# Hybrid DeltaNet and attention layer on one core: modulation rows moved, bias corners set once, paired products in the inverse, the last head's output spread out

## The chip, the cores and the metric

The kernel runs on one core of a Trainium2 chip. The metric is the device time of one execution in microseconds (us). Three executions of the kernel before took 2202.82, 2208.03 and 2638.72 us; the median is 2208.03 us. The profiled execution took 2206.4 us, of which the trace covers a span of 2204.7 us.

## The reference: what is computed

One layer on 1024 tokens of width 1024, all in float32:

```python
mod = (silu(c) @ w_ada + b_ada)                    # 6 x 1024: shift, scale, gate, twice
h = x * (1 + scale_t) + shift_t
proj = h @ w_in                                    # 9232 columns
o_a = gated_deltanet(q, k, v, z, beta, a)          # 8 heads of 128, chunks of 64
o_b = chunk_band_attention(q, k, v, rel_bias)      # 16 heads of 64, own chunk and 8 before
merged = gate_a * (o_a @ w_branch_a) + gate_b * (o_b @ w_branch_b)
x = layernorm(alpha * x + gate_t * (merged @ w_o))
h = x * (1 + scale_f) + shift_f
u_gate, u_val = split(causal_dwconv(h @ w_up) + b)
x = layernorm(alpha * x + gate_f * ((silu(u_gate) * u_val) @ w_down))
```

The DeltaNet heads solve a unit lower triangular system for each chunk of 64 rows. The attention adds a relative-position bias to the scores; a frame sees no key outside its band, which the kernel expresses by a large negative number (`NEG`) in two 64x64 corners of the bias tile.

## The kernel before, in words

Every large product is made from two parts of each operand, a high part (the float32 value cast to fp32r) and a low part (what the cast left). A product is three matmuls: high x high, low x high, high x low. So each weight block that is loaded into a buffer `raw` (a ring of three, 512 KB each) is cast on ScalarE (ACT), which gives `wh`, and its low part `wl` is the difference, taken on GpSimd (POOL, lines 177 and 188) or VectorE (DVE, line 177). All loads and stores are issued by SyncE (SP) in program order.

The stages, in order of time:

- 0 to about 100 us: the first part of the modulation, the layer's input, the first projections.
- About 100 to 800 us: the eight DeltaNet heads. The loop over h = 0 to 6 (line 934) runs, for head h, the solve and the recurrence, while `feed(h + 1)` (line 681) makes the next head's projections, short convolution, Gram matrices and the rows that the solve reads; it also makes some blocks of the merge gates (`gate_block`) and of the attention's q and k (`qk_block`), taken from the iterator `gates`. `feed` yields after each few matmuls and says how many units they were. The loop's `waves` are streams with a position in units: a wave is run when the feed has come so far. Waves are `stage_inverse` (line 767, four pieces), `stage_chain` (line 811, the recurrence) and `stage_out` of the head before (line 846; tiles `pt`, `sz`).
- `stage_solve` (line 744) is forward substitution on VectorE in 32 rows: a product (line 751) and a reduction (line 753) per row on a tile that the ring calls FT, a transpose (line 755), then copies of blocks (line 763) and transposes (line 765). `stage_inverse` joins the 32x32 blocks into 64x64 ones by small matmuls: `pxt` and `py` for the 32x32 blocks, then `pzz` and `pT`, sixteen of 64x64 each. There are two small products per step for `pxt`, which lie in two different quarters of the partitions.
- `mod_rows(cb)` (line 898) makes 512 of the later modulation's 4096 columns: four loads of 512 KB of `w_ada` into the ring `raw`, eight VectorE operations that sum them over the rows (lines 907 and 909), one matmul `pmod` with ones, a bias row and a store. Rows of 512 are numbered 0 to 7. `feed(h + 1)` makes row h in its second half, and in the fourth head row 7 as well (`HM = 3`).
- About 800 to 1310 us: the last DeltaNet head and then the attention's 64 groups (16 heads of 4 groups, the loop of `g` at line 1261). Both are filled with a second stream, `fills`: the remaining q and k blocks (`pqk`), the values (`pv`), the load of branch A's input (`branch_a_in`, line 1064: eight loads of 512 KB with cast and low part), and branch A's eight weight blocks (`branch_a(j)`, line 1074). `FILL` and `SHARE` say how many units lie between the steps of a group.
- A group's scores `ps` get the bias and their exponentials' sums on VectorE and ACT (lines 1153 to 1159), GpSimd divides by the sum (line 1160, tile G, widths 128 to 640), TensorE transposes (`pp`), ACT casts and VectorE makes the low part `pl` (line 1182), and TensorE makes the output `po`.
- `Head.bias` (line 993) loads one head's bias into a tile of a ring of two (G as well), in two pieces (line 997), and sets two corners to `NEG` by GpSimd (lines 998 and 999). `Head.keys` (line 980) casts the first head pair's keys twice on ACT, once to each half of the partitions (lines 982 and 983), and takes the low part on VectorE (line 984).
- About 1240 to 1350 us: the rest of branch A (`pbr`). With j = 5, 6 and 7 the attention's output is read back from `ob_d` through `raw`, cast and split. Then branch B (line 1304, `mm_fm`, `pbr` at line 286), the output product, the normalisation, the up product (line 1515, seven products in place of eight) and the down product (line 1669), to 2205 us.

Instructions are put in order by a scheduler with a timeline of its own; in the loop of the heads, in the last head and in the attention the matmuls are kept in the order in which the program has them (`lane.pinned`), and every engine keeps the order that the build gives it.

Of the kernel before, what the change touches and what calls it, by code (L numbers as in the profile page):

```python
# [17 lines left out]
P = 128  # L18
S = 1024
D = 1024  # L20
NK = 8
# [16 lines left out]
HM = 3  # L38
# [7 lines left out]
MS = 6  # L46
FILL = (120, 124, 100, 112, 125, 130, 140, 110)
# [90 lines left out]
def hybrid_layer(  # L138
# [542 lines left out]
    def feed(h, n_gates, mods):  # L681
# [36 lines left out]
        if mods[1:]:  # L718
            run(mod)
            mod = mod_rows(mods[1])  # L720
            next(mod)
# [22 lines left out]
    def stage_solve(h, c):  # L744

        fa = c["fa"]
        ft = ring("ft", [P, 8, 32])
        POOL.tensor_copy(ft, tt0)
        for i in range(1, 32):
            pr = ring("pr", [P, 8, 32])  # L750
            DVE.tensor_tensor(pr[:, :, 0:i + 1], ft[:, :, 0:i + 1],  # L751
                              fa[:, i:i + 1, 0:i + 1].to_broadcast([P, 8, i + 1]), ALU.mult)
            DVE.tensor_reduce(ft[:, :, i:i + 1], pr[:, :, 0:i + 1], AX.X, ALU.add, negate=True)  # L753
        fr = ring("pr", [P, 8, 32])
        DVE.transpose(fr.rearrange("p c j -> p (c j)"), ft.rearrange("p c j -> p (c j)"))
        for b in (1, 3, 0, 2):
            for q in range(4):
                dst = dd[B[b], :, 32 * b + 8 * q:32 * b + 8 * q + 8]
                s_ = fr[B[q], :, 8 * b:8 * b + 8].rearrange("p c t -> p t c")
                if q % 2:  # L760
                    ACT.copy(dst, s_)
                else:
                    DVE.tensor_copy(dst, s_)
        for b in (1, 3, 0, 2):
            DVE.transpose(dt_[B[b], :, B[b]], dd[B[b], :, B[b]])

    def stage_inverse(h, c):
# [31 lines left out]
        pz = ibank("pzz", 64)  # L799
        for u in range(NT):  # L800
            lane.matmul(pz[lo_, u], am[:, u, lo_], am[:, u, hi_], start=True, stop=True)
        ACT.activation(zd[lo_], pz[lo_], AF.Copy, scale=-1.0)
        POOL.memset(am[hi_, :, lo_], 0.0)
        yield
        pT = ibank("pT", 64)
        for u in range(NT):
            lane.matmul(pT[lo_, u], dd[:, u, lo_], zd[:, u], start=True, stop=True)
        DVE.tensor_copy(am[lo_, :, hi_], pT[lo_])
# [89 lines left out]
    def mod_rows(cb):  # L898

        C = slice(2 * D + 512 * cb, 2 * D + 512 * cb + 512)  # L900
        acc = ring("gt", [P, 512])
# [12 lines left out]
        row = ring("gt", [P, 512])[0:1, :]  # L914
# [5 lines left out]
    gates = iter([*range(1, 2 * NK), *((i,) for i in EP)])  # L920
# [13 lines left out]
    for h in range(HA - 1):  # L934
        fill, done = feed(h + 1, GA[h], (h, HA - 1)[:1 + (h == HM)]), 0
# [6 lines left out]
        i0 = INV0 if h else INV00  # L942
        waves += [(inv, i0 + INVS * i) for i in range(4)]
# [18 lines left out]
    vts, ma, keys_low = {}, {}, []  # L962

    class Head:
# [15 lines left out]
        def keys(self, N, src, at):  # L980
            kh, kl = self.kh, self.kl
            ACT.copy(kh[at:at + 64, N], src)
            ACT.copy(kh[64 - at:P - at, N], src)
# [9 lines left out]
        def bias(self):  # L993
            bt = self.bt = ring("bt", [P, 640])
            src = rel_d[self.h].rearrange("r s -> (r s)")[127:127 + 767 * P].rearrange("(p s) -> p s", p=P)
            for c in (slice(384, 640), slice(0, 384)):
                SP.dma_start(bt[:, c], src[:, c])
            POOL.memset(bt[0:64, 576:640], NEG)
            POOL.memset(bt[64:128, 0:64], NEG)
# [65 lines left out]
    def branch_a_in():  # L1065

        def body(_):
            for k in range(NK):
                load_split(oahk[k], oalk[k], oa_d[k], ACT, POOL if k in OL else DVE)
# [4 lines left out]
    def branch_a(j):  # L1074

        def body(w):
            ma[j] = place(MA[j], [P, S], F32, "ma")
            for n in range(2):
# [5 lines left out]
                DVE.scalar_tensor_tensor(gt_, gt_, 1.0, ps, ALU.add, ALU.mult)  # L1084
            for k in {5: (0, 1), 6: (2, 3, 4), 7: (5, 6, 7)}.get(j, ()):
# [146 lines left out]
    waves = [(older, OUT0 + OUTS * i) for i in range(3)]  # L1232
# [12 lines left out]
    for i, (stream, at_) in enumerate(waves):  # L1245
        if i == 7:
            group("GA", "G", 4096)
            head(0).bias()
# [11 lines left out]
    done, owed = 0, None  # L1260
    for g in range(8 * NK):
# [12 lines left out]
        if g == 0:  # L1274
            seq += [lambda: wave(last, PC)] * 3
# [521 lines left out]
```

## Time and profile before

| what | value |
|---|---|
| median of three executions | 2208.03 us |
| profiled execution | 2206.4 us |
| its span | 2204.7 us |
| granted TensorE clock, mean | 0.992 |
| TensorE busy | 2123.3 us, 11561 matmuls |
| VectorE busy | 1451.7 us |
| ScalarE busy | 981.7 us |
| GpSimd busy | 488.3 us |
| bytes moved | 258.78 MB, 38.0% of 16 DMA engines |

The page gives busy time by engine, then the span in 40 slices, the DMA queues, the chain of work that ended last, and the costliest groups by line. The view of waits lists, for each engine, what its idle time ended on: total us, times, longest. A timeline row is start, duration, engine, line, operation, output and inputs, and in brackets the idle time just before it with what ended it. Names are those of the program's buffers, so that many tiles of one ring share a name: `G` is the scores, the bias tiles and small pieces of the solve, `GT` the gates and the modulation's sums, `FT` the solve's rows, and later the ring `gb`.

### The profile page before, as it was taken

How to read it: one execution, taken by the hardware profiler on the slowest of the kernel's cores; microseconds unless marked ns; L12 is line 12 of the kernel's file. 1: busy time of each engine (PE TensorE's matmuls, PEld its weight loads, DVE VectorE, ACT ScalarE, POOL GpSimd, SP SyncE). 2: the span in 40 equal slices, each digit the busy share in tenths (PEclk: the TensorE clock that was granted, in tenths of full speed). 3: DMA queues.
4: the chain of work that ended last, by engine and by line, in shares of the span. 5: the costliest groups of instructions: out<-in, count | busy, mean ns of one | idle time of the engine just before them, and what ended most of it. 6: DMA issues, size and time to landing. Idle time of an engine off the chain costs nothing.

```text
span 2204.7 us, 32006 instructions
## 1 busy us (share of the span) xinstructions
PE 2123.3 (96%) x11561; PEld 1775.4 (81%) x11561; DVE 1451.7 (66%) x3112; ACT 981.7 (45%) x2129; POOL 488.3 (22%) x466
## 2 busy tenths in 40 slices
PE   7999999999999999998999899999999999999998
PEld 5787888877887878888888788888788888888886
DVE  6478586777767734655655553457997888875654
ACT  4544443443434433555555542234654444452331
POOL 0233223222232222332333423300120000000000
PEclk9999999999999999999999999999999999999999
DMA  9242324333234124535454633342232222275540
GB/s 291 75 130 63 117 75 118 127 92 115 82 106 129 51 75 134 146 95 134 121 142 131 170 122 97 112 133 87 85 97 86 68 86 77 96 261 207 172 153 38
DMA packets 239520, 258.78 MB, mean 117 GB/s; under 512 B 21818, under 2 KB 188147, under 8 KB 239363
## 3 DMA queue, kind: packets, MB, share of 16 engines
q1 hardware_dynamic: 239283, 256.72, 38.0%
q8 instruction: 91, 1.49, 0.3%
q14 instruction: 66, 0.54, 0.1%
q10 hardware_dynamic: 80, 0.03, 0.0%
HBM read 204.22 MB, written 58.76 MB: 119 GB/s over the span
## 4 chain that ended last, share of the span: by engine, by line
PE 78%; DVE 10%; DMA 5%; ACT 3%; POOL 2%; issue 2%; SPq 1%; DVEq 0%; ACTq 0%; POOLq 0%
PE pup L1515 17%; PE pdn L1669 11%; PE pqkv L528 9%; PE pqk L528 6%; PE pwo L1357 4%; PE pgt L528 4%; PE pbr L286 4%; PE pv L528 4%; PE pbr L528 4%; PE po L528 3%; PE pz L528 3%; DVE FT L751 2%; PE ps L528 2%; PE pp L528 2%; DVE FT L753 1%
## 5 line engine op out<-in xcount | busy, mean ns | idle before, releaser
L1515 PE MATMUL pup<-hh,wop 128*128 128x512 f32 x704 | 224.3, 390 | 0.4 <-ACT G L1552 0.4
L1515 PE MATMUL pup<-t,wop 128*128 128x512 f32 x792 | 189.5, 392 | 1.2 <-DVE cc L1556 0.7
L177 POOL TENSOR_TENSOR wl<-raw,wh 128x1024 fp32r<-128x1024 f32 x55 | 131.7, 2397 | 265.0 <-ACT wh L174 242.5
L1515 PEld LDWEIGHTS pup<-t,wop 128*128 128x128 f32 x792 | 148.6, 188 | 34.7 <-DVE cc L1556 1.1
L1669 PE MATMUL pdn<-dop,dop 128*128 128x512 f32 x696 | 161.6, 391 | 0.0
L1515 PEld LDWEIGHTS pup<-hh,wop 128*128 128x128 f32 x704 | 132.2, 188 | 29.1 <-ACT G L1552 0.8
L1669 PEld LDWEIGHTS pdn<-dop,dop 128*128 128x128 f32 x696 | 130.6, 188 | 28.3
L528 PE MATMUL pqkv<-hh,wh 128*128 128x512 f32 x352 | 144.0, 410 | 0.0
L528 PE MATMUL pqkv<-hl,wh 128*128 128x512 f32 x352 | 141.0, 401 | 0.0
L528 PE MATMUL pqkv<-hh,wl 128*128 128x512 f32 x352 | 140.8, 400 | 0.0
L1160 POOL TENSOR_SCALAR G<-G,ST 128x640 f32<-128x640 f32 (+4 forms) x128 | 86.4, 676 | 240.8 <-DVE ST L1159 180.3
L1515 PE MATMUL pup<-hl,wop 128*128 128x512 f32 x352 | 137.2, 390 | 0.0
L1557 POOL TENSOR_TENSOR cc<-cc,G 128x512 f32<-128x512 f32 x22 | 44.4, 2018 | 375.4 <-DVE G L1539 352.3
L1157 ACT ACTIVATE G<-G,ST 128x640 f32<-128x640 f32 (+4 forms) x128 | 89.3, 698 | 67.5 <-DVE ST L1153 66.5
L751 DVE TENSOR_TENSOR FT<-FT,G 128x16 f32<-128x16 f32 (+30 forms) x248 | 103.7, 418 | 12.8 <-POOL G L650 5.5
L528 PE MATMUL pqk<-hh,wh 128*128 128x512 f32 x256 | 106.8, 417 | 3.6 <-DVE GT L879 3.6
L174 ACT CAST wop<-wr 128x512 fp32r<-128x512 f32 x104 | 61.6, 620 | 97.4 <-DVE wr L1497 57.5
L528 PE MATMUL pqk<-hl,wh 128*128 128x512 f32 x256 | 104.7, 409 | 0.0
L528 PE MATMUL pp<-ident,G 128*128 128x128 f32 x480 | 78.8, 276 | 26.6 <-POOL G L1160 20.8
L528 PE MATMUL pqk<-hh,wl 128*128 128x512 f32 x256 | 104.2, 407 | 0.0
L528 PE MATMUL pgt<-hh,wh 128*128 128x512 f32 x240 | 98.2, 409 | 0.0
L528 PE MATMUL pgt<-hh,wl 128*128 128x512 f32 x240 | 97.6, 407 | 0.0
(403 smaller groups left out, 5665.8 us busy)
## 6 DMA issues: line engine op xcount, KB each, us to landing
raw<-in_w_in_dram SPq DMA_DIRECT2D x72, 512.0 KB
wr<-in_w_up_dram SPq DMA_DIRECT2D x44, 512.0 KB
dwr<-in_w_down_dram SPq DMA_DIRECT2D x44, 512.0 KB
raw<-in_w_ada_dram SPq DMA_DIRECT2D x32, 512.0 KB
qk_d<-FT SPq DMA_DIRECT2D x72, 128.0 KB
wa<-in_w_ada_dram SPq DMA_DIRECT2D x32, 256.0 KB
gates_d<-GT SPq DMA_DIRECT2D x32, 256.0 KB
g_d<-G SPq DMA_DIRECT2D x15, 512.0 KB
```

What stands on the lines that cost most here:

```text
L174: he.copy(h, src)
L177: return le.tensor_tensor(l, src, f(h), ALU.subtract).ins
L286: i = PE.matmul(ps, a[:, k, :], r[k][:, 512 * n:512 * n + 512], start=(k == 0 and a is wh and r is rh), stop=(k == NK - 1 and a is wl))
L528: r = getattr(PE, op)(*args, **kw)
L751: DVE.tensor_tensor(pr[:, :, 0:i + 1], ft[:, :, 0:i + 1], fa[:, i:i + 1, 0:i + 1].to_broadcast([P, 8, i + 1]), ALU.mult)
L753: DVE.tensor_reduce(ft[:, :, i:i + 1], pr[:, :, 0:i + 1], AX.X, ALU.add, negate=True)
L1157: ACT.activation(sb[:, 0:n], sb[:, 0:n], AF.Exp, bias=mx[:, nb - 1:nb], scale=-1.0, accum_out=mx[:, 2:3])
L1160: POOL.tensor_scalar(sb[:, 0:n], sb[:, 0:n], mx[:, 3:4], 0.0, ALU.mult, ALU.add)
L1357: PE.matmul(ps[n], a[:, t, k, :], wo[k][b][:, 512 * n:512 * n + 512], start=(k == 0 and a is mh and b == 0), stop=(k == NK - 1 and a is ml))
L1515: i = PE.matmul(ps, a[:, u, k, :], b[v][k], start=(new and k == 0 and u == 0 and v == 0), stop=(k == 3 and u == 1), skip_group_check=not new)
L1557: self.later(7, lambda: POOL.tensor_tensor(o, o, self.t, ADD))
L1669: PE.matmul(ps[n], self.g[:, u, i * P:i * P + P], self.w[v][:, 512 * n:512 * n + 512], start=(first and u == 0 and v == 0), stop=(last and ...
```

## The change

There are eight edits.

1. **Modulation.** `feed(h + 1)` makes row h - 1 for h = 1 to 6, so no row in head 1's feed, and one in each later one (0 to 5). Rows 6 and 7 are made in branch A: row 6's loads and sums start after block j = 4 and its matmul and store after j = 5, row 7 after j = 6 and j = 7. Their sums lie in the ring `gb`.
2. **Order of the blocks.** `gates` gives q and k blocks 4 and 12 after gate block 3 (in head 1's feed) and no longer at the end (in head 7's feed).
3. **Block copies.** `stage_solve` ends with the transpose of line 755; what follows (lines 756 to 765) is `stage_blocks`, a wave at position 0 of the head's own loop (22 units before the inverse for head 0).
4. **Paired products.** `pzz` and `pT` write the even of their sixteen products to partitions 0 to 63 and the odd ones to 64 to 127. Each result is then copied in two halves of 64 x 4 x 64, for `pzz` by two ACT operations in place of one, for `pT` by one on ACT and one on VectorE.
5. **Bias corners.** `bias()` issues four loads that leave the corners out, in place of two loads and two GpSimd operations. The corners of the ring's two tiles are set once, before head 0's bias.
6. **Keys.** The second ACT cast of `keys` is replaced by a copy by DMA from the first half.
7. **Last head's output.** Eight units of fill come before the attention's loop, and in group 0 the three pieces of the last `stage_out` stand between pieces of fill of four units, after the first turn.
8. **Low parts.** `branch_a_in` takes the low parts in two pieces of 512 columns (`cuts=2`).

```diff
-HM = 3
+HEAD0 = 8
@@ feed
-        if mods[1:]:
-            run(mod)
-            mod = mod_rows(mods[1])
-            next(mod)
@@ stage_solve, stage_blocks
-        fr = ring("pr", [P, 8, 32])
+        fr = c["fr"] = ring("pr", [P, 8, 32])
         DVE.transpose(fr.rearrange("p c j -> p (c j)"), ft.rearrange("p c j -> p (c j)"))
+
+    def stage_blocks(h, c):
+        fr = c["fr"]
         for b in (1, 3, 0, 2):
...
             DVE.transpose(dt_[B[b], :, B[b]], dd[B[b], :, B[b]])
+        yield
@@ stage_inverse
-        pz = ibank("pzz", 64)
+        sides = (lo_, hi_)
+        def pairs(name):
+            return mtile(nm(name), "i")[:, 0:256].rearrange("p (t d) -> p t d", d=64)
+        pz = pairs("pzz")
         for u in range(NT):
-            lane.matmul(pz[lo_, u], am[:, u, lo_], am[:, u, hi_], start=True, stop=True)
-        ACT.activation(zd[lo_], pz[lo_], AF.Copy, scale=-1.0)
+            lane.matmul(pz[sides[u % 2], u // 2], am[:, u, lo_], am[:, u, hi_], start=True, stop=True)
+        for i in range(2):
+            ACT.activation(zd[lo_, i::2], pz[sides[i]], AF.Copy, scale=-1.0)
...
-        pT = ibank("pT", 64)
+        pT = pairs("pT")
         for u in range(NT):
-            lane.matmul(pT[lo_, u], dd[:, u, lo_], zd[:, u], start=True, stop=True)
-        DVE.tensor_copy(am[lo_, :, hi_], pT[lo_])
+            lane.matmul(pT[sides[u % 2], u // 2], dd[:, u, lo_], zd[:, u], start=True, stop=True)
+        ACT.copy(am[lo_, 0::2, hi_], pT[lo_])
+        DVE.tensor_copy(am[lo_, 1::2, hi_], pT[hi_])
@@ mod_rows: acc and row from ring(key)
-    def mod_rows(cb):
+    def mod_rows(cb, key="gt"):
@@ gates and the loop of the heads
-    gates = iter([*range(1, 2 * NK), *((i,) for i in EP)])
+    gates = iter([1, 2, 3, *((i,) for i in EP), *range(4, 2 * NK)])
-        fill, done = feed(h + 1, GA[h], (h, HA - 1)[:1 + (h == HM)]), 0
+        fill, done = feed(h + 1, GA[h], (h - 1,) if h else ()), 0
+        waves = [(stage_blocks(h, cs[h]), 0)] + waves if h else [(stage_blocks(h, cs[h]), i0 - 22)]
@@ Head.keys, Head.bias
-            ACT.copy(kh[64 - at:P - at, N], src)
+            SP.dma_start(f(kh[64 - at:P - at, N]), f(kh[at:at + 64, N]))
-            for c in (slice(384, 640), slice(0, 384)):
-                SP.dma_start(bt[:, c], src[:, c])
-            POOL.memset(bt[0:64, 576:640], NEG)
-            POOL.memset(bt[64:128, 0:64], NEG)
+            for r, c in ((lo_, slice(384, 576)), (hi_, slice(384, 640)), (lo_, slice(0, 384)), (hi_, slice(64, 384))):
+                SP.dma_start(bt[r, c], src[r, c])
@@ branch_a_in, branch_a
-                load_split(oahk[k], oalk[k], oa_d[k], ACT, POOL if k in OL else DVE)
+                load_split(oahk[k], oalk[k], oa_d[k], ACT, POOL if k in OL else DVE, cuts=2)
+            if j in (4, 6):
+                mods_late.append(mod_rows(j // 2 + 4, "gb"))
+                next(mods_late[-1])
+            if j in (5, 7):
+                run(mods_late[-1])
@@ last head and group 0
-    waves = [(older, OUT0 + OUTS * i) for i in range(3)]
+    waves = [(stage_blocks(h, cs[h]), 0)] + [(older, OUT0 + OUTS * i) for i in range(3)]
-        if i == 7:
+        if i == 8:
             group("GA", "G", 4096)
+            for o in AT["bt"]:
+                corner = place(o, [P, 640], F32, "bt")
+                POOL.memset(corner[0:64, 576:640], NEG)
+                POOL.memset(corner[64:P, 0:64], NEG)
             head(0).bias()
+    fill_to(HEAD0)
-            seq += [lambda: wave(last, PC)] * 3
+            seq = [head(1).bias, T[0], lambda: fill_to(done + 4), lambda: wave(last, PC), lambda: fill_to(done + 4),
+                   lambda: wave(last, PC), lambda: wave(last, PC), lambda: fill_to(done + 4)]
```

**GpSimd's order in the attention.** This is GpSimd's queue from the corners of the third head's bias on, before and then after. `L1160` of before is `L1173` after; `wl` is a weight's low part.

```order
L998 MEMSET G_7233 64x64
L188 TENSOR_TENSOR wl_8245<-raw_8246,wh_8244 128x512 x2
L999 MEMSET G_7233 64x64
L1160 TENSOR_SCALAR G_7233<-G_7233,ST_7002 128x128
L1160 TENSOR_SCALAR G_7233<-G_7233,ST_7002 128x256
L1160 TENSOR_SCALAR G_7233<-G_7233,ST_7002 128x384
L1160 TENSOR_SCALAR G_7233<-G_7233,ST_7002 128x512
L1160 TENSOR_SCALAR G_7233<-G_7233,ST_7002 128x640 x2
L188 TENSOR_TENSOR wl_8252<-raw_8253,wh_8251 128x512 x2
L1160 TENSOR_SCALAR G_7233<-G_7233,ST_7002 128x640 x2
L998 MEMSET G_7233 64x64
L1160 TENSOR_SCALAR G_7233<-G_7233,ST_7002 128x128
```

```order
L188 TENSOR_TENSOR wl_8223<-raw_8224,wh_8222 128x512 x2
L1173 TENSOR_SCALAR G_7207<-G_7207,ST_6954 128x128
L1173 TENSOR_SCALAR G_7207<-G_7207,ST_6954 128x256
L1173 TENSOR_SCALAR G_7207<-G_7207,ST_6954 128x384
L1173 TENSOR_SCALAR G_7207<-G_7207,ST_6954 128x512
L1173 TENSOR_SCALAR G_7207<-G_7207,ST_6954 128x640 x2
L188 TENSOR_TENSOR wl_8230<-raw_8231,wh_8229 128x512 x2
L1173 TENSOR_SCALAR G_7207<-G_7207,ST_6954 128x640 x2
L1173 TENSOR_SCALAR G_7207<-G_7207,ST_6954 128x128
```

The two corner operations no longer stand ahead of a division or between two of them; the low parts and the divisions keep their order.

**TensorE's order at the last head's output.** TensorE's queue where group 0 begins, before and then after: `pqk` is fill, `pp` the transposes of group 0's probabilities, `pt` the last head's output transposed.

```order
L528 MATMUL pp_7814<-ident,G_7233 128x128 x3
L528 MATMUL pqk_7792<-hl,wh_7673 128x512
L528 MATMUL pqk_7792<-hh,wl_7674 128x512
L528 MATMUL pt_7822<-ident,at_6667 128x128 x4
L528 MATMUL pqk_7792<-hh,wh_7673 128x512
L528 MATMUL pqk_7792<-hl,wh_7673 128x512
L528 MATMUL pt_7830<-ident,at_6667 128x128 x4
```

```order
L528 MATMUL pp_7797<-ident,G_7207 128x128 x3
L528 MATMUL pqk_7770<-hh,wh_7651 128x512
L528 MATMUL pqk_7770<-hl,wh_7651 128x512
L528 MATMUL pqk_7770<-hh,wl_7652 128x512
L528 MATMUL pqk_7770<-hh,wh_7651 128x512
L528 MATMUL pt_7807<-ident,at_6643 128x128 x4
L528 MATMUL pqk_7770<-hl,wh_7651 128x512
L528 MATMUL pqk_7770<-hh,wl_7652 128x512
L528 MATMUL pqk_7770<-hh,wh_7651 128x512
L528 MATMUL pqk_7770<-hl,wh_7651 128x512
L528 MATMUL pt_7817<-ident,at_6643 128x128 x4
```

Between `pp` and the first `pt` stand four matmuls of fill in place of two, and between the two `pt` four in place of two; the eight units of `HEAD0` stand further ahead.

**SyncE's order at the end of branch A.** SyncE's queue up to branch B's first weight (the last row), before and then after; `raw` is the ring of three, `raw<-ob_d` the attention's output read back.

```order
L182 DMA raw_12827<-ob_d 128x1024
L1083 DMA ma_12909<-gates_d 128x512
L1083 DMA ma_12772<-gates_d 128x512 x2
L1083 DMA ma_12842<-gates_d 128x512 x2
L182 DMA raw_12897<-ob_d 128x1024
L1083 DMA ma_12909<-gates_d 128x512
L182 DMA raw_12831<-ob_d 128x1024
L1209 DMA ob_d<-ob_12227 128x512
L182 DMA raw_12964<-ob_d 128x1024
L1364 DMA B_1563_12677<-mod_d 16x128
L182 DMA raw_12837<-in_w_branch_a_dram 128x8x128
L182 DMA raw_12978<-in_w_branch_b_dram 128x8x128
```

```order
L912 DMA raw_12908<-in_w_ada_dram 128x2x512
L912 DMA raw_12912<-in_w_ada_dram 128x2x512
L925 DMA mod_d<-FT_12664 1x512
L912 DMA raw_12916<-in_w_ada_dram 128x2x512
L923 DMA FT_12664<-in_b_ada_dram 1x512
L182 DMA raw_12920<-ob_d 128x1024
L182 DMA raw_12924<-ob_d 128x1024
L182 DMA raw_12928<-ob_d 128x1024
L182 DMA raw_12992<-ob_d 128x1024
L182 DMA raw_12996<-ob_d 128x1024
L182 DMA raw_13000<-ob_d 128x1024
L182 DMA raw_13006<-in_w_branch_b_dram 128x8x128
```

Row 7's loads of `w_ada` now stand between block j = 7 and six of the reads of `ob_d`, row 6's stand ahead of block j = 6 (earlier than these rows), and all reads of `ob_d` stand ahead of branch B's first weight, where four of the eight followed it before.

More of the change, by code (lines that the diff above doesn't have):

```diff
@@ L896, in gate_block @@
         return halves("pgt", GC + j * P, use, pend.pop("g", None))
-    def mod_rows(cb):
+    def mod_rows(cb, key="gt"):
         C = slice(2 * D + 512 * cb, 2 * D + 512 * cb + 512)
-        acc = ring("gt", [P, 512])
+        acc = ring(key, [P, 512])
         for k0 in range(0, NK, 2):
@@ L913, in mod_rows @@
         lane.matmul(pr_, ones, acc, start=True, stop=True)
-        row = ring("gt", [P, 512])[0:1, :]
+        row = ring(key, [P, 512])[0:1, :]
         SP.dma_start(row, b_ada[:, C])
@@ L961, in hybrid_layer @@
     oalk = [oal[:, k, :] for k in range(NK)]
-    vts, ma, keys_low = {}, {}, []
+    vts, ma, keys_low, mods_late = {}, {}, [], []
     class Head:
@@ L994, in bias @@
             bt = self.bt = ring("bt", [P, 640])
+            lo_, hi_ = slice(0, 64), slice(64, P)
             src = rel_d[self.h].rearrange("r s -> (r s)")[127:127 + 767 * P].rearrange("(p s) -> p s", p=P)
-            for c in (slice(384, 640), slice(0, 384)):
-                SP.dma_start(bt[:, c], src[:, c])
-            POOL.memset(bt[0:64, 576:640], NEG)
-            POOL.memset(bt[64:128, 0:64], NEG)
+            for r, c in ((lo_, slice(384, 576)), (hi_, slice(384, 640)), (lo_, slice(0, 384)), (hi_, slice(64, 384))):
+                SP.dma_start(bt[r, c], src[r, c])
     heads = {}
```

## The prediction, as it was put on record

> **What bounds the kernel now.** I read the page first, its span and busy times:
>
> ```profile
> span 2204.7 us, 32006 instructions
> ...
> PE 2123.3 (96%) x11561; PEld 1775.4 (81%) x11561; DVE 1451.7 (66%) x3112; ACT 981.7 (45%) x2129; POOL 488.3 (22%) x466
> ```
>
> TensorE (PE) is busy 96% of the span, and the change gives it as many matmuls as before. So a gain can be of two kinds only: idle time on TensorE (2204.7 - 2123.3 = 81 us, the start included), or matmuls that overlap. The view of waits says what TensorE's idle time ended on (total us, times, longest):
>
> ```profile
> PE pp L528 <- POOL G L1160: 20.8, 18, 3.7
> ...
> PE pvn L528 <- DVE FT L753: 3.9, 1, 3.9
> PE pt L528 <- DVE pl L1182: 3.7, 1, 3.7
> PE pkk L528 <- DVE kd L613: 3.7, 1, 3.7
> PE pqk L528 <- DVE GT L879: 3.6, 1, 3.6
> ...
> PE pvn L528 <- DVE vs L820: 1.8, 1, 1.8
> PE pp L528 <- POOL G L999: 1.8, 1, 1.8
> PE pv L528 <- DVE kl L984: 1.7, 1, 1.7
> ```
>
> All of these end on VectorE or GpSimd, and each row stands where an edit touches the program. None is long: the largest single wait is 3.9 us, so the change is a sum of small terms, and I read the timeline around each.
>
> **The change part by part.** All terms are against the profiled 2206.4 us, the span and 1.7 around it.
>
> *Bias corners, -8.* GpSimd's waits between 890 and 1215 us, and its timeline at one of these places, show it standing at a corner until the bias has landed:
>
> ```profile
> POOL G L998 <- DMA G<-rel_d: 27.8, 12, 4.5
> POOL G L999 <- DMA G<-rel_d: 8.2, 11, 1.9
> ```
> ```profile
> 943.22 0.14 POOL L998 MEMSET G<- 64x64 f32 x1 [4.07 <-DMA G<-rel_d]
> 944.60 0.15 POOL L999 MEMSET G<- 64x64 f32 x1 [1.24 <-DMA G<-rel_d]
> 944.84 0.82 POOL L1160 TENSOR_SCALAR G<-G,ST 128x128 f32<-128x128 f32 x2
> ```
>
> In the first two rows are 36.0 us of GpSimd's idle time. At 944.84 two divisions follow the corner at once: they were ready and queued behind it. I followed each gap of TensorE before a `pp` back to GpSimd's queue; nine have a corner ahead of the division, of which these are the first and the last:
>
> ```profile
> 892.78 0.89 PE L528 MATMUL pp<-ident,G 128*128 128x128 f32 x3 [0.32 <-POOL G L1160]
> ...
> 1210.62 0.66 PE L528 MATMUL pp<-ident,G 128*128 128x128 f32 x4 [0.29 <-POOL G L1160]
> ```
>
> The nine make 11.1 us, out of the 22.6 of the two `pp` rows above. That is the gain if nothing else is late there; about half of it, 5, if the divisions' own inputs come just behind. I take 8, nearer the whole, as divisions ran back to back behind the corner. Each of sixteen heads issues two loads more on SyncE. SyncE has idle time between the heads, and only an issue that stands ahead of an urgent load costs: +0.5 (0 to +2).
>
> *Paired products, -7.4.* The sixteen products of `pzz`, and the thirty-two smaller ones of `pxt`, in TensorE's timeline, and the durations of a single one in the view by tile:
>
> ```profile
> 186.69 0.70 PE L528 MATMUL pxt<-G,am 128*32 128x32 f32 x32
> ...
> 194.75 1.15 PE L528 MATMUL pzz<-am 128*64 128x64 f32 x16
> ```
> ```profile
> L528 PE MATMUL pzz<-am x128: 222/222/270, 194.7 to 797.3; 128*64 128x64 f32 x128
> ```
> ```profile
> L528 PE MATMUL pxt<-G,am x256: 196/196/217, 186.7 to 788.8; 128*32 128x32 f32 x128
> ```
>
> The last `pzz` alone takes 0.222 us, so fifteen others start within 0.93 us, 62 ns each, for 64 columns. `pxt` alternates between two parts of the partitions: (0.70 - 0.196) / 31 = 16 ns each for 32 columns, where 62 per 64 would give 31. Two run at once there. If pairs of `pzz` and `pT` do the same, each step loses 0.46 us: two steps in eight heads, 16 x 0.46 = 7.4. If they don't, nothing. I take the whole, since `pxt` is the nearest row. The extra ACT operation lies beside fourteen units of fill that stand between two steps; without that cover it would cost TensorE some 0.3 us a head.
>
> *Modulation: -3 in head 1, -3 around the fourth head.* One row is eight operations of this kind (the group of line 909 by tile), and head 1's feed has none after the change:
>
> ```profile
> L909 DVE SCALAR_TENSOR_TENSOR GT<-raw,csil,GT x56: 728/751/2773, 138.2 to 706.9; 128x512 f32<-128x512 f32 x56
> ```
> ```profile
> 174.18 1.80 DVE L763 COPY G<-FT 32x64 f32<-32x64 f32 x8
> ```
>
> 8 x 0.75 = 6.0 us go from VectorE ahead of `kd`, for which `pkk` waits 3.7. They could take all of it. But the solve's block copies (1.80, and transposes behind them), which now come just after `kd`, may then come just before: -3 (-1 to -3.7). In the fourth head two rows become one. The waits there are `pvn`'s 3.9 and 1.8; VectorE ahead of the first, and GpSimd at that time:
>
> ```profile
> 479.46 2.40 DVE L751 TENSOR_TENSOR FT<-FT,G 128x64 f32<-128x64 f32 x1
> 481.79 2.33 DVE L731 TENSOR_SCALAR SM<-SM 128x8 f32<-128x8 f32 x1
> ...
> 484.53 0.23 DVE L751 TENSOR_TENSOR FT<-FT,G 128x72 f32<-128x72 f32 x1
> ```
> ```profile
> 479.24 4.85 POOL L177 TENSOR_TENSOR wl<-raw,wh 128x1024 fp32r<-128x1024 f32 x2 [2.36 <-ACT wh L174]
> ```
>
> The first wait is made by two operations that took ten times their usual time beside GpSimd's low parts. With less queued before, VectorE may meet them elsewhere or not: -3, half of 5.7 (0 to -5.7).
>
> *Blocks 4 and 12, -3, and the keys, -1.* `pqk`'s 3.6 us wait is for VectorE's operation of such a block, behind the solve's transposes; the keys' second cast is the second row:
>
> ```profile
> 774.72 1.37 DVE L765 STREAM_TRANSPOSE G<-G 32x256 f32<-32x256 f32 x3
> 776.12 0.69 DVE L879 TENSOR_TENSOR GT<-pqk,GT 128x512 fp32r<-128x512 f32 x1
> ```
> ```profile
> 809.61 0.58 ACT L983 CAST kh<-pqk 64x512 fp32r<-64x512 f32 x1
> ```
>
> The block moves to head 1's feed, and the wait goes with it: -3 (0, if the next block meets the same transposes, to -3.6). `kl` starts only after the cast of 0.58 us, and `pv` waits 1.7 for it: -1 (0 to -1.7). The copy by DMA that replaces the cast is read by scores much later.
>
> *Last head's output, -1.4.* `pt` waits 3.7 us for `pl`, which VectorE reaches late. Four more matmuls ahead of the second `pt`, at the 0.23 us in which the large ones follow one another, give 0.9, and eight units of fill further ahead some of the rest; VectorE's heap of work stays: -1.4 (+1 to -3.7).
>
> *Low parts of branch A's input, -3.* TensorE's waits between 1200 and 1240 us, then GpSimd's and VectorE's timelines there:
>
> ```profile
> PE pp L528 <- POOL G L1160: 6.8, 4, 3.7
> PE pp L528 <- DVE pl L1182: 1.9, 1, 1.9
> ```
> ```profile
> 1216.18 2.41 POOL L177 TENSOR_TENSOR hl<-raw,hh 128x1024 fp32r<-128x1024 f32 x1 [0.19 <-ACT hh L174]
> ...
> 1224.46 2.52 POOL L188 TENSOR_TENSOR wl<-raw,wh 128x512 fp32r<-128x512 f32 x2 [0.34 <-ACT wh L185]
> ```
> ```profile
> 1217.36 2.32 DVE L177 TENSOR_TENSOR hl<-raw,hh 128x1024 fp32r<-128x1024 f32 x1 [0.53 <-ACT hh L174]
> ...
> 1221.14 1.23 DVE L177 TENSOR_TENSOR hl<-raw,hh 128x1024 fp32r<-128x1024 f32 x1 [0.52 <-ACT hh L174]
> ```
>
> These are 8.7 us. Two pieces cost GpSimd 0.1 us more than one (2.52 against 2.41) and let a division in after 1.26. That shortens a wait by up to 1.2, for each of four: -3 (+1, if the pieces stand back to back anyway, to -8).
>
> VectorE's low part took 2.32 us beside GpSimd's and 1.23 alone. The Trainium skill's "GPSIMD Engine Reference" (Specifications) says that GpSimd shares its SBUF interfaces with VectorE and contends with VectorE instructions that have two SBUF inputs; these rows agree. By that rule two pieces keep the whole contention, this term would be 0, and the sum 3 higher.
>
> *Late modulation, +2.5.* Rows 6 and 7 put sixteen VectorE operations (12 us, for which it has room) and eight loads into the end of branch A. The attention's last row, the reads of `ob_d`, branch B's first low part, and its first matmul:
>
> ```profile
> 1313.04 0.43 DVE L1206 TENSOR_TENSOR ob<-po,FT 64x256 f32<-64x256 f32 x1
> ```
> ```profile
> 1318.92 6.62 SPq L182 DMA_DIRECT2D raw<-ob_d  x3
> ```
> ```profile
> 1327.78 2.44 POOL L177 TENSOR_TENSOR wl<-raw,wh 128x1024 fp32r<-128x1024 f32 x1 [8.88 <-ACT wh L174]
> ```
> ```profile
> 1347.89 0.63 PE L286 MATMUL pbr<-ob,wh 128*128 128x512 f32 x2
> ```
>
> Branch B's weight is ready at 1327.78 + 2.44 = 1330.2 and wanted at 1347.9, 17.7 us later. After the change sixteen loads, that weight the last, pass the ring of three once the sums can start, at 1313, when the attention's last rows leave the tiles in which the sums lie. Three `ob_d` issues stand 6.62 / 2 = 3.3 us apart while two slots are free, so a slot turns over in 6.6 and three slots pass a load each 2.2: 16 x 2.2 = 35, with 2.4 for the low part 37.5, against 1347.9 - 1313 = 35 at hand: 2.5 late. With two slots 16 x 3.3 = 53, and 20 late; 0 if the sums start earlier. I take 2.5, as the slot that branch B's weight blocks now is free by then.
>
> The sum: -8 + 0.5 - 7.4 - 3 - 3 - 3 - 1 - 1.4 - 3 + 2.5 = -26.8; 2206.4 - 26.8 = 2179.6. The median shown is 1.6 us above the profiled time, too little to correct for: forecast **2179.6**.
>
> **The rivals.**
>
> *The waits move on.* What TensorE waits for is late by another name. For it: half of the 20.8 us of `pp` has no corner in it, and the operations of 2.4 us at 479 are no order's fault. Against: ready divisions stood behind the corners. Then the pairs and the corners' lower end stay: 2206.4 - 7.4 - 5 + 3 = 2197.
>
> *All named waits go.* 11.1 + 7.4 + 3.7 + 5.7 + 3.6 + 1.7 + 3.7 + 8 = 44.9, and the late rows are free: 2161.5. Against: VectorE and GpSimd would have to be in time everywhere, with all their work kept.
>
> *The pairs don't overlap.* `pxt` has smaller tiles than they. 2179.6 + 7.4 = 2187.
>
> *Late modulation starves branch B.* This one ends slower than before. If the ring passes one load at a time, 6.6 us each, sixteen take 106 and the weight comes 106 + 2.4 - 35 = 73 us late: 2179.6 - 2.5 + 73 = 2250. It is slower than before once the delay exceeds the other terms' 29.3, at (35 - 2.4 + 29.3) / 16 = 3.9 us a load. For it: sums, casts and low parts share the ring in one fixed order, so one late consumer holds all. Against: the reads at 1318.92 pass each 3.3 us with a slot blocked.
>
> **How the numbers follow.** The forecast has 0.58 (its own range 2169 to 2190), the waits that move on 0.20, all that go 0.12, pairs without overlap 0.06, the starved branch 0.04. For eight in ten the range is 2163 to 2197: below it lies most of the second rival, above it part of the first and the last. A measurement of this kernel tells about 2% from no change, which is 44.2 us from 2208.03: under 2163.9 counts as faster, which is a little over half of the second rival, 0.07; over 2252 is some of the last, 0.01; 0.92 lies between.
>
> **What would show it.** The corners: no idle time of GpSimd that ends on `rel_d`, and `pp`'s waits for divisions down from 20.8 to about 13. The pairs: sixteen `pzz` in about 0.7 us, not 1.15. Head 1: `pkk`'s wait under 2 us. `pqk`'s 3.6 gone. The late rows: branch B's first matmul waits 0 to 8 us for its weight. The prediction is wrong if TensorE's idle time falls by less than 10 us, if `pzz` keeps its 1.15, or if a wait of over 10 us stands at branch B's start.

## The result and the profile after

The changed kernel took 2179.68 us (median of four, 2176.09 to 2180.29) against 2207.66 us before: a ratio of 0.9877, with a 95% interval of 0.9857 to 0.9898. One of the four executions before was slow (2638.72 us), and the ratio leaves it out. The profiled execution took 2179.74 us, its span is 2178.0 us, 26.7 less than before. The forecast total was met almost to the microsecond; its terms were not, as the runs below show.

The page's first lines of the changed kernel, span and busy times:

```profile
span 2178.0 us, 32044 instructions
## 1 busy us (share of the span) xinstructions
PE 2109.8 (97%) x11561; PEld 1765.2 (81%) x11561; DVE 1447.3 (66%) x3117; ACT 984.9 (45%) x2141; POOL 483.1 (22%) x441
```

TensorE has the same 11561 matmuls and is busy 13.5 us less (2123.3 to 2109.8). Its idle time, span less busy time, is down by 13.2 (81.4 to 68.2). So half of the gain is matmul time and half is waits. What it waits for now:

```profile
PE pp L528 <- POOL G L1173: 16.2, 13, 6.7
PE pks L528 <- DVE SA L843: 4.7, 6, 1.9
...
PE pqk L528 <- ACT GT L901: 3.3, 1, 3.3
PE pbr L286 <- ACT wh L174: 3.1, 1, 3.1
PE pkk L528 <- DVE kd L613: 2.7, 1, 2.7
PE pp L528 <- DVE pl L1195: 2.2, 3, 1.0
PE pT L528 <- ACT G L809: 2.2, 1, 2.2
PE pt L528 <- DVE pl L1195: 2.1, 1, 2.1
```

`pvn`'s waits of 3.9 and 1.8 us are gone. Five things were not foreseen: one `pp` now waits 6.7 us, where the longest before was 3.7; `pqk` waits 3.3 in place of 3.6, for another releaser; `pT` has a wait of 2.2 of its own; `pks`, with 3.0 us before and none over 0.6, now has 4.7 and one of 1.9; and `pbr` waits 3.1 at the start of branch B. The pairs in head 0, in TensorE's timeline (start, duration, and in brackets the idle time before):

```profile
188.47 0.69 PE L528 MATMUL pzz<-am 128*64 128x64 f32 x16 [1.49 <-ACT am L798]
...
194.71 0.69 PE L528 MATMUL pT<-G 128*64 128x64 f32 x16 [2.18 <-ACT G L809]
```

Sixteen products take 0.69 us, not 1.15: 0.46 less, as forecast.

**A wait costs more than itself.** The rest of the matmul time that went (13.5 less 16 x 0.46 = 7.4, so some 6 us) is no work that was taken out. About half of it can be followed to TensorE's clock. In the stretches where the traces show a granted clock of 0.50, TensorE was busy for 29.2 us before and for 22.4 after, and half of the difference, 3.4 us, is what the slow clock took. The other 2.7 us these traces don't resolve. The windows view of before, just after `pkk`'s wait of 3.7 us ended at 171.6, and after `pzz`'s of 1.8 us at 712.4 (after the stretch's length stands each engine's busy time, then the clock granted to TensorE, the third number from the end), and TensorE's timeline behind the first:

```profile
171.60:175.00 3.40, 3.38 (x12) 3.09 (x13) 3.27 (x11) 2.01 (x6) 2.00 (x2) 0.50 0.05 16
```
```profile
713.40:717.00 3.60, 3.60 (x13) 2.87 (x12) 0.03 (x1) 1.75 (x3) 0.52 (x1) 0.53 0.55 162
```
```profile
174.35 0.63 PE L528 MATMUL pqkv<-hh,wl 128*128 128x512 f32 x1
174.78 0.63 PE L528 MATMUL pqkv<-hh,wh 128*128 128x512 f32 x1
...
178.18 0.39 PE L528 MATMUL pqkv<-hh,wh 128*128 128x512 f32 x1
178.41 0.39 PE L528 MATMUL pqkv<-hl,wh 128*128 128x512 f32 x1
```

TensorE is busy all the time, but at half the clock: the same matmuls start 0.43 us apart at 174 and 0.23 apart at 178. Over 3.4 us that loses 3.4 x (1 - 0.5) = 1.7 us behind the wait. Behind this first wait the slow clock held on to 177.6, which makes 3.0 us. The prediction counted waits alone.

The Trainium skill's "TensorE: Matmul & The Clock Gate" (What's actually happening) says that TensorE's clock is halved after an idle window of about 3.4 us and comes back after a busy one, and that the window runs free of the kernel. These rows agree in ratio and length. They don't agree that a whole idle window is needed: the second wait here is 1.8 us, about half of one.

### The profile page after: what moved, and what is told of

Read it like the earlier page. It is cut to its first block, busy times and chain, and to the rows that moved or that the text cites. A ratio compares the mean times of both kernels' runs of the same rounds, so it can differ in the third digit from the quotient of the medians.

```text
span 2178.0 us, 32044 instructions
## 1 busy us (share of the span) xinstructions
PE 2109.8 (97%) x11561; PEld 1765.2 (81%) x11561; DVE 1447.3 (66%) x3117; ACT 984.9 (45%) x2141; POOL 483.1 (22%) x441
## 4 chain that ended last, share of the span: by engine, by line
PE 81%; DVE 10%; ACT 3%; DMA 3%; POOL 1%; issue 1%; SPq 1%; DVEq 0%; ACTq 0%; POOLq 0%
PE pup L1534 17%; PE pdn L1688 11%; PE pqkv L528 9%; PE pqk L528 7%; PE pv L528 4%; PE pbr L286 4%; PE pwo L1376 4%; PE po L528 3%; PE pgt L528 3%; PE pz L528 3%; DVE FT L747 3%; PE pbr L528 3%; PE ps L528 2%; PE pp L528 2%; DVE FT L749 2%
## 5 line engine op out<-in xcount | busy, mean ns | idle before, releaser
L1173 POOL TENSOR_SCALAR G<-G,ST 128x640 f32<-128x640 f32 (+4 forms) x128 | 85.4, 668 | 260.1 <-DVE ST L1172 196.9
L747 DVE TENSOR_TENSOR FT<-FT,G 128x16 f32<-128x16 f32 (+30 forms) x248 | 97.2, 392 | 11.1 <-POOL G L650 3.7
L528 PE MATMUL pp<-ident,G 128*128 128x128 f32 x480 | 78.0, 276 | 20.2 <-POOL G L1173 16.2
```

Of the source, the lines that this page charges most:

```text
L528: r = getattr(PE, op)(*args, **kw)
L747: DVE.tensor_tensor(pr[:, :, 0:i + 1], ft[:, :, 0:i + 1], fa[:, i:i + 1, 0:i + 1].to_broadcast([P, 8, i + 1]), ALU.mult)
L1173: POOL.tensor_scalar(sb[:, 0:n], sb[:, 0:n], mx[:, 3:4], 0.0, ALU.mult, ALU.add)
```

## The experiments

All but the last undo one edit of the changed kernel or vary it, so an edit was worth, beside the others, what its undoing costs. Of the longer edits a few lines stand here, with `...` where lines are left out. The medians come from several chips, so each stands with its ratio to the kernel before on the same chip; the changed kernel's is 0.9877 (0.9857 to 0.9898).

**Bias corners again per head** (edit 5 undone).

```diff
-            for r, c in ((lo_, slice(384, 576)), (hi_, slice(384, 640)), (lo_, slice(0, 384)), (hi_, slice(64, 384))):
-                SP.dma_start(bt[r, c], src[r, c])
+            for c in (slice(384, 640), slice(0, 384)):
+                SP.dma_start(bt[:, c], src[:, c])
+            POOL.memset(bt[0:64, 576:640], NEG)
+            POOL.memset(bt[64:128, 0:64], NEG)
...
-            for o in AT["bt"]:
-                corner = place(o, [P, 640], F32, "bt")
-                POOL.memset(corner[0:64, 576:640], NEG)
-                POOL.memset(corner[64:P, 0:64], NEG)
```

> The changed kernel with the bias corners set again for each head (two loads and two GpSimd operations, edit 5 undone), all else as changed. The prediction's theory: GpSimd stands at the corners again and TensorE's transposes pp wait behind, so the time rises by 8 us from 2179.7 (5 to 11), to about 2188, and pp's waits on the division line rise from 16.2 us by about as much. Rival theory (the waits move on): the divisions' inputs come just behind the bias, the time rises by less than 3 us. A third reading: the wait that remains at the clock (a wait that costs half the clock for 3.4 us behind it) makes it rise by more than the waits themselves.

Measured: 2191.65 us, ratio 0.9938 (0.9923 to 0.9953): 12 us over the changed kernel's median, more than the 8 of the prediction's theory and far from the rival's 3. The waits of TensorE on the division line rise only from 16.2 to 20.0:

```profile
PE pp L528 <- POOL G L1174: 20.0, 17, 5.6
```

What the rise of waits doesn't show, one place does. GpSimd's timeline, TensorE's wait, and the clock there:

```profile
997.26 0.14 POOL L1007 MEMSET G<- 64x64 f32 x1 [1.53 <-DMA G<-rel_d]
997.38 0.37 POOL L1174 TENSOR_SCALAR G<-G,ST 128x128 f32<-128x128 f32 x1
999.71 0.15 POOL L1008 MEMSET G<- 64x64 f32 x1 [1.97 <-DMA G<-rel_d]
999.94 2.48 POOL L188 TENSOR_TENSOR wl<-raw,wh 128x512 fp32r<-128x512 f32 x2
1002.40 0.48 POOL L1174 TENSOR_SCALAR G<-G,ST 128x256 f32<-128x256 f32 x1
```
```profile
1002.94 0.69 PE L528 MATMUL pp<-ident,G 128*128 128x128 f32 x2 [3.29 <-POOL G L1174]
```
```profile
1000.00:1003.50 3.50, 0.56 (x3) 0.57 (x4) 0.03 (x1) 0.00 (x0) 2.88 (x3) 0.55 0.55 163
1003.50:1007.00 3.50, 3.50 (x18) 3.50 (x18) 1.21 (x5) 1.55 (x4) 0.59 (x1) 0.50 0.52 150
```

The corner waits 1.97 us for its DMA, the low part behind it takes 2.48, and only then comes the division: a wait of 3.29 us, and half the clock for the 3.5 us behind it (1.75 lost). The third reading held: with the corners, waits are longer where they meet a low part, and the clock adds to them. Over the whole attention, from its first `po` to its last, this kernel takes 437.3 us and the changed one 425.9 (426.6 in a second trace): some 11 us, of which about 5 are idle time of TensorE and 4 to 5 the slow clock. The profiled spans differ by 14.8; the rest lies outside the attention, for the most part ahead of it, where the slow clock took 5 us more.

**The pairs undone** (edit 4).

```diff
-            lane.matmul(pz[sides[u % 2], u // 2], am[:, u, lo_], am[:, u, hi_], start=True, stop=True)
+            lane.matmul(pz[lo_, u], am[:, u, lo_], am[:, u, hi_], start=True, stop=True)
...
```

> The changed kernel with pzz and pT one behind the other (edit 4 undone). The prediction's theory: TensorE's own time rises by 7.4 us (sixteen steps of 0.46), to about 2187, since nothing waits for these steps. Rival: the shorter steps only brought waits closer, so part of the 7.4 is taken up by TensorE's waits for the copies behind the pairs, and the time rises by less than 4 us.

Measured: 2189.03 us, ratio 0.9929 (0.9912 to 0.9945), 9 us more than the changed kernel's median; its profiled span is 2184.9, 6.9 more than the changed one's. The steps have 1.15 us again:

```profile
190.41 1.15 PE L528 MATMUL pzz<-am 128*64 128x64 f32 x16
```

From the second head's `pxt` to the seventh's each loop takes 87.6 to 87.8 us in place of 86.7 to 86.9: 0.9 a loop, two steps of 0.46. The rival (waits take up the gain, under 4 us) falls as to the sum; 7.4 stands within what either number tells. It was right in head 0: the waits of 1.5 us for `pzz` and of 2.2 for `pT` are none and 1.5 here.

**The modulation as before** (edit 1 undone, `HM = 3`, no late rows).

```diff
...
-        fill, done = feed(h + 1, GA[h], (h - 1,) if h else ()), 0
+        fill, done = feed(h + 1, GA[h], (h, HA - 1)[:1 + (h == HM)]), 0
...
```

> The changed kernel with the modulation as before (row h in head h + 1's feed, row 7 also in the fourth; no late rows), all other edits kept. The prediction's terms: +3 in head 1, +3 at the fourth head, -2.5 at branch B, so +3.5 to about 2183. What the trace of the changed kernel suggests: the fourth loop alone rises by about 8 us (9.5 us shorter after the change, 0.9 of it by pairs), branch B's start gains 4.8, so +4 to +6, to about 2185, with a wait of pvn of some 4 us back at 480 us. If the fourth loop's gain came from another edit (blocks' order or block copies), that loop stays at 86.8 us and the time falls by about 5 us to 2175.

Measured: 2183.03 us, ratio 0.9889 (0.987 to 0.9908): about what both readings gave. The stretches tell them apart. The first `pxt` of the fourth and the fifth head, here and then in the changed kernel:

```profile
428.65 0.70 PE L529 MATMUL pxt<-G,am 128*32 128x32 f32 x32
...
523.75 0.70 PE L529 MATMUL pxt<-G,am 128*32 128x32 f32 x32
```
```profile
425.14 0.70 PE L528 MATMUL pxt<-G,am 128*32 128x32 f32 x32
...
511.97 0.70 PE L528 MATMUL pxt<-G,am 128*32 128x32 f32 x32
```

The loop takes 95.1 us with two rows and 86.8 with one: 8.3 us, where the prediction had 3 and at most 5.7. TensorE's waits in that loop with two rows, and the clock at the first:

```profile
PE pvn L529 <- DVE FT L754: 3.9, 1, 3.9
PE pvn L529 <- DVE vs L833: 1.5, 1, 1.5
```
```profile
482.00:486.00 4.00, 3.80 (x15) 3.19 (x15) 3.62 (x13) 3.98 (x5) 0.99 (x1) 0.57 0.48 131
```

Both waits come back, 5.4 us, and 4.0 x (1 - 0.57) = 1.7 behind the first; the other 1.2 is put down, without a run for it, to the second row's own matmuls and small gaps. At branch B's start this kernel has no wait; there the changed one pays, for its late rows, a part of that gain.

**One late row** (row 6 in head 1's feed, row 7 late).

```diff
-        fill, done = feed(h + 1, GA[h], (h - 1,) if h else ()), 0
+        fill, done = feed(h + 1, GA[h], (h - 1,) if h else (6,)), 0
...
-            if j in (4, 6):
-                mods_late.append(mod_rows(j // 2 + 4, "gb"))
+            if j == 4:
+                mods_late.append(mod_rows(7, "gb"))
...
```

> The changed kernel with row 6 of the modulation in head 1's feed and only row 7 late (in branch A's blocks 4 and 5). If the two late rows are what makes branch B wait (3.1 us and a slow clock behind it), one late row clears the wait: -5 us there; head 1 gets 6 us of VectorE work back, which by the prediction costs 3 us: about 2178, and by the trace (head 1's waits are now later, for the inverse) anything from 0 to 5: 2175 to 2180.

Measured: 2176.47 us, ratio 0.9867 (0.9847 to 0.9887), not told apart from the changed kernel by the interval. The wait for branch B's weight is gone from its list of waits, but one of 2.1 us stands at the end of branch A in its place, and `pkk`'s is 3.7 again:

```profile
PE pkk L528 <- DVE kd L613: 3.7, 1, 3.7
...
PE pbr L528 <- DVE ma L1092: 2.1, 1, 2.1
```

**Single low parts** (edit 8 undone).

```diff
-                load_split(oahk[k], oalk[k], oa_d[k], ACT, POOL if k in OL else DVE, cuts=2)
+                load_split(oahk[k], oalk[k], oa_d[k], ACT, POOL if k in OL else DVE)
```

> The changed kernel with branch A's input's low parts in one piece of 1024 columns (edit 8 undone). The prediction's theory: +3 (-1 to +8), since a division waits up to 1.2 us longer behind GpSimd's piece. Rival theory: in the changed kernel the longest wait there, 6.7 us, ends on a division behind a branch A weight's low part and on VectorE's sums, which pieces of the input do not move; the stretch between the 400th and the 500th po stays at 82 to 87 us and the time within 1 us.

Measured: 2171.78 us, ratio 0.9848 (0.9825 to 0.9871). Undoing this edit makes the kernel faster: some 6 us by the ratios, whose intervals overlap, and 7.9 by the medians. No single time of this kernel (2169.62 to 2175.38) reaches the lowest of the changed one. Neither theory had the sign. The longest wait of `pp` falls from 6.7 to 1.7:

```profile
PE pp L528 <- POOL G L1173: 10.7, 14, 1.7
```

In the changed kernel, VectorE had the sum for the 512-wide division at 1190.73, but GpSimd has a weight's low part ahead of it, and TensorE's `pp` behind:

```profile
1190.73 0.15 DVE L1172 RECIPROCAL ST<-ST 128x1 f32<-128x1 f32 x1
```
```profile
1194.80 2.48 POOL L188 TENSOR_TENSOR wl<-raw,wh 128x512 fp32r<-128x512 f32 x2 [7.90 <-ACT wh L185]
1197.26 1.47 POOL L1173 TENSOR_SCALAR G<-G,ST 128x512 f32<-128x512 f32 x2
```
```profile
1198.00 1.12 PE L528 MATMUL pp<-ident,G 128*128 128x128 f32 x4 [6.73 <-POOL G L1173]
```

ACT cast that weight only at 1193.67, when its load had come. With single pieces GpSimd's order is the other way round, the division first:

```profile
1194.49 0.69 POOL L1173 TENSOR_SCALAR G<-G,ST 128x512 f32<-128x512 f32 x1 [4.35 <-DMA raw<-in_w_branch_a_dram]
1195.57 1.29 POOL L188 TENSOR_TENSOR wl<-raw,wh 128x512 fp32r<-128x512 f32 x1 [0.39 <-ACT wh L185]
```

The first row names a DMA as what ended the wait, but VectorE's reciprocal for this division ends at 1194.40, just ahead of it; TensorE's `pp` behind waits 0.25 us.

The clock in the six microseconds from 1198 on was 0.56 in the changed kernel; with single pieces it was whole from 1191 to 1204:

```profile
1198.00:1204.00 6.00, 6.00 (x21) 0.56 1.09 226
```
```profile
1191.00:1204.00 13.00, 12.04 (x66) 1.00 1.12 268
```

**Two pieces on VectorE alone, and on GpSimd alone.** Two kernels cross the two suspects, the pieces and the order. GpSimd has three of the eight low parts (`OL = (1,3,5)`) and VectorE five; the two expectations below and the prediction counted four for GpSimd.

```diff
-                load_split(oahk[k], oalk[k], oa_d[k], ACT, POOL if k in OL else DVE, cuts=2)
+                load_split(oahk[k], oalk[k], oa_d[k], ACT, POOL if k in OL else DVE, cuts=1 if k in OL else 2)
```

> The changed kernel with GpSimd's four low parts of branch A's input in one piece and VectorE's four in two. In its order GpSimd still has the low part of branch A's first weight ahead of the 512-wide division. Theory (order): the 6 us that two pieces cost come from that place in GpSimd's order, where the division waits for a weight's load; so this kernel keeps the long wait of pp (over 4 us) and the stretch from the 400th to the 500th po takes 84 to 88 us. Rival (pieces on GpSimd): its two pieces beside VectorE's are what costs; this kernel is then like the one with single pieces, about 80 us there, and 6 us faster in all than the changed kernel.

The second has `cuts=2 if k in OL else 1`.

> The changed kernel with GpSimd's four low parts in two pieces and VectorE's four in one. In its order GpSimd has the 512-wide division ahead of the low part of branch A's first weight. Theory (order): no wait of pp over 3 us there, the stretch from the 400th to the 500th po takes about 80 us, and the time is 6 us under the changed kernel's. Rival (pieces on GpSimd): 84 to 88 us there, as in the changed kernel.

Measured: 2177.06 us, ratio 0.9881 (0.9858 to 0.9905), and 2180.79 us, ratio 0.9894 (0.987 to 0.9917). TensorE's waits from 1140 to 1260 us, first with pieces on VectorE alone, then on GpSimd alone:

```profile
PE pp L528 <- POOL G L1173: 8.8, 6, 3.8
```
```profile
PE pp L528 <- POOL G L1173: 10.7, 6, 5.0
```

From the 400th to the 500th `po` of the attention (counted from 0), by their starts in TensorE's timeline, they take 82.8 and 86.8 us (86.4 changed, 79.6 with single pieces). The first kernel lies between its two forecasts. The second came out as the rival (pieces on GpSimd) had it; by the theory of order it should have been quick. Its GpSimd queue shows why:

```profile
1197.92 2.49 POOL L188 TENSOR_TENSOR wl<-raw,wh 128x512 fp32r<-128x512 f32 x2 [2.87 <-ACT wh L185]
1200.39 0.80 POOL L1173 TENSOR_SCALAR G<-G,ST 128x640 f32<-128x640 f32 x1
```

There the second weight's low part, waiting for its load, stands ahead of a 640-wide division, and `pp` waits 5.0 us behind. It holds the division for 1.5 us only, since the reciprocal for it ends at 1198.86. More was lost in ScalarE's queue, where the exponential that the reciprocal needs stands behind the cast of the same weight:

```profile
1196.80 1.04 ACT L185 CAST wh<-raw 128x1024 fp32r<-128x1024 f32 x1 [3.48 <-DMA raw<-in_w_branch_a_dram]
1197.75 0.82 ACT L1170 ACTIVATE G<-G,ST 128x640 f32<-128x640 f32 x1
```

VectorE's part of that group was done at 1194.98. So in all three kernels with pieces a ready operation stands behind one that waits for a weight's load, in the first two in GpSimd's queue and here for the greater part in ScalarE's. Seven other kernels of this section keep edit 8. Six of them, and the changed kernel's second trace, have a weight's low part ahead of the ready 512-wide division too, and their longest `pp` waits are 4.1 to 7.1 us; the one with the corners undone is as with pieces on GpSimd alone (5.6). The two kernels with single pieces have the division ahead, and 1.7 and 1.3. That the order is the cause is argued from these queues; a kernel with two pieces and with every division ahead was not made.

**The other edits undone.** Blocks 4 and 12 back in head 7's feed (`gates = iter([*range(1, 2 * NK), *((i,) for i in EP)])`):

> The changed kernel with blocks 4 and 12 back in head 7's feed (edit 2 undone). The prediction's theory: the wait of 3.6 us for such a block's operation on VectorE comes back and the time rises by 3 us (0 to 3.6). Rival, from the trace of the changed kernel: the same matmuls still wait 3.3 us, now for a gate block's operation on ACT, so that only the name of the releaser changes and the loop before the last pxt stays at 81 us within 0.5.

Measured: 2182.16 us, ratio 0.9895 (0.9871 to 0.9919). From the seventh head's `pxt` to the eighth's it takes 83.8 us against 81.1. The size is the prediction's, the mechanism isn't: the waits there, undone and then in the changed kernel, are

```profile
PE pqk L528 <- DVE GT L887: 3.6, 1, 3.6
PE pzz L528 <- ACT am L798: 1.3, 1, 1.3
```
```profile
PE pqk L528 <- ACT GT L901: 3.3, 1, 3.3
```

`pqk` only changed its releaser, as the rival said; what went is `pzz`'s 1.3 us and 0.3 of `pqk`'s. The last 1.0 is the slow clock behind `pqk`, which held for 6.8 us here and for 3.4 in the changed kernel. It held for 6.8 with one late row as well, and there the same loop takes 82.2 us, so this part isn't the edit's.

The last head's output in one piece again (`seq += [lambda: wave(last, PC)] * 3`, no `HEAD0`):

> The changed kernel with the last head's output in one piece after group 0 (edit 7 undone). The prediction's theory: pt's wait goes from 2.1 back to about 3.7 us, the time rises by 1.4 us (-1 to +3.7). Rival: a wait this long also costs a slow clock behind it in both forms, so that the time stays within 1 us.

Measured: 2180.85 us, ratio 0.9885 (0.986 to 0.991), no difference that this can tell; `pt` waits 3.7 us in place of 2.1: 1.6 is seen as a wait, where 1.4 was forecast. The slow clock stands behind it in both, for 3.4 us, as the rival said. The block copies at the end of the solve again (edit 3 undone):

> The changed kernel with the solve's block copies at the end of the solve again (edit 3 undone). The prediction gave this edit no price of its own but for head 0, where copies may come just before the last kd and take part of the modulation's gain. By that, undoing it leaves heads 2 to 7 at 86.8 us a loop and moves the first two heads by -2 to +3 us. Rival: the copies' later place is what removed waits of pvn and pzz in the later heads; then loops of the later heads lengthen by 1 us or more each.

Measured: 2177.58 us, ratio 0.9872 (0.9845 to 0.9899). From the second head's `pxt` to the seventh's the loops stay at 86.7 to 86.8 us, and the first two end within 0.7 us of the changed kernel's. Edit 3 is worth nothing that these runs can show; the rival falls.

**Both improvements together** (single pieces and one late row), beside the changed kernel on the same chip.

> The changed kernel with single pieces (edit 8 undone) and with row 6 of the modulation in head 1's feed, so that only row 7 is late. If the two are separate, the gains add: 6 us of the pieces and 2 to 4 of the late row, about 2169. If the two lie in one stretch and the wait at branch B's start only moves, no better than single pieces alone: about 2173.

> The changed kernel itself once more, for comparison on the same chip with the others of this call: 2178 to 2181 by the first four runs. If its 10 us at the low clock near 1193 us and its short first two heads were one execution's luck, single stretches differ by 2 to 4 us from the first trace while the total stays within that.

Measured: 2170.92 us (2170.28 to 2173.04), ratio 0.9853 (0.983 to 0.9875), against 2177.25 us (2176.07 to 2181.05), ratio 0.9878 (0.9852 to 0.9904), for the changed kernel: 6.3 us less, with no overlap of the single times, though the intervals of the ratios overlap. It is faster than both kernels, but by the single pieces almost alone: 2171.78 without the early row. The late row's gain at branch B goes back in head 1, where `pkk` waits 3.6 again. In the changed kernel's second trace the 10 us at the low clock near 1193 were 6.8, while the stretch there took 86.1 us against 86.4: the wait is the kernel's, the clock behind it varies.

## Why the prediction was right, and where not

| step | forecast | what the runs showed |
|---|---|---|
| corners, with more issues | -8 + 0.5 | -12 (medians), -11 in the attention; direction right, size too small |
| pairs | -7.4 | -7.4 by the steps; -7 to -9 by the undone kernel |
| double row, fourth head | -3 (0 to -5.7) | -8.3 |
| head 1 without a row | -3 | not resolved: 253.3 to 254.8 us up to the second head's `pxt` with a row, 250.5 to 253.8 without (pairs kept); `pkk` from 3.7 to 2.7, but `pT` (2.2), `pks` (1.9) and `pzz` (1.5) wait instead |
| blocks 4 and 12 | -3 | -2.7, by another wait than the one named; 1.0 of it is the clock's luck |
| keys | -1 | not run alone; `pv`'s wait went from 1.7 to 0.9 |
| last head's output | -1.4 | -1.6 as a wait, not resolved in the total |
| low parts in two pieces | -3 | +6 (ratios) |
| late rows | +2.5 | a wait of 3.1 (2.3 in the second trace) and half a clock behind it, 1.7: +4.8 |

That the total was right is luck, since errors cancelled: corners and the double row gave some 10 us more than forecast (4.5 and 5.3), low parts and late rows took some 11 more (9 and 2.3). The table's entries needn't add up to the 26.7, since edits share stretches.

Of the prediction's signs, three came: no idle time of GpSimd ends on `rel_d`, `pzz` takes 0.69 us, and branch B's first matmul waits 3.1. Three didn't: `pp`'s waits for divisions fell to 16.2 and not to about 13, `pkk` waits 2.7 and not under 2, and `pqk`'s wait stayed.

The step of the sum that failed is the low parts: "let a division in after 1.26" supposed that the pieces interleave with divisions, and no division came between any two of them in GpSimd's queue. The prediction looked at durations and not at GpSimd's new order, in which a waiting low part stands ahead of the division. The same reasoning was applied to the corners, where it was right: what a queue's head waits for is paid by all behind it. The sentence of the Trainium skill on the shared SBUF interfaces ("GPSIMD Engine Reference", Specifications), which would have set this term to 0, was nearer but not the cause found: the long wait was for a load.

In head 1 the term of -3 failed by a rival of the prediction, the waits that move on. TensorE's waits between 100 and 260 us add up to 9.4 us in the changed kernel and to 8.0 with the modulation as before: `pkk`'s went down by 0.9, and the waits that came behind it took that and more.

Two sizes were off for one reason: the double row and the late rows were priced by their waits alone. The double row's two waits did go whole, which had been put at half for fear that the slow VectorE operations would meet others; and behind the longer wait and branch B's stood 1.7 us of half clock. The pace of the late loads was right: the fifteen loads into `raw` ahead of branch B's first weight are issued from 1278.35 to 1313.30, 2.3 us each, where the prediction had 2.2. Of the rivals, the waits that move on were right in single places (head 1, `pqk`, `pbr`), not in the sum.

## What to carry to other kernels

Before an edit is priced by durations, print the order of the engines that it touches and look at what stands ahead of the instruction that others wait for: an operation that waits for a load must not stand ahead of one that is ready. A wait of 3 us on a TensorE that is otherwise always busy should be priced at nearly 5. And a total that comes out right proves none of its terms; only undoing the edits one by one did that here.

## What was not expected of the hardware

In the traces of before, of the changed kernel and of the variants, the clock fell to half, for 3.4 us or a multiple of it, at every TensorE wait of 3 us or more, but for those of the first 15 us. Below that it depends: it fell after 1.76 us at 712.4 before, not after 1.80 at 513 or 2.04 at 1103 there, nor after the changed kernel's 2.72 for `pkk` at 166.9, while with the corners undone it fell behind that one. In the changed kernel it fell at waits as short as 1.87 us (`pks` at 215.6) and 1.75 (`pp` at 992.3), and a wait of 2.1 for `pt` brought it there but not with pieces on VectorE alone. What sets it off below 3 us stays open here. The same wait can also cost differently from execution to execution, as near 1193.
